# One encoder layer on one core: another way of starting it, with the norm's gain spread by the matrix engine, loads from two queues, and another order of casts, copies and transposes

## The chip, the cores and the metric

The kernel runs on one core of a Trainium2 chip. A core has five engines that each work through an instruction stream of their own, in order: PE (TensorE, matrix multiplication), DVE (VectorE), ACT (ScalarE), POOL (GpSimd) and SP (SyncE, which here only issues DMA transfers; ACT can issue them too). They are tied together by semaphores: an instruction can wait until another engine, or a transfer, has counted up. PE reads operands from the on-chip memory SBUF and writes to the accumulator banks in PSUM; DVE and ACT read PSUM, and POOL in this kernel works in SBUF alone. The metric is the device time of one execution in microseconds (us), the median of the runs.

## The reference

One layer over a sequence of 1024 tokens of width 1024, all in float32. What matters here is its beginning:

```python
h = rmsnorm(x, g_mix)          # x / sqrt(mean(x*x) + eps) * g, for each token
z = h @ w_in                   # columns: 512 pooling | 1024 q | 1024 k | 1024 v
y_pool = pool_mixer(z[:, :512], ...)
y_attn = diff_attention(q, k, v, ...)          # 8 heads
gates  = sigmoid(h @ w_gate + b_gate)
merged = gates[:, :1024] * (y_pool @ w_branch_pool) + gates[:, 1024:] * (y_attn @ w_branch_attn)
x = x + merged @ w_out
x = x + square(relu(rmsnorm(x, g_ffn) @ w_up)) @ w_down
```

Every token needs its normalised row `h` before anything can be multiplied, and head 0 needs its 384 columns of `w_in` (128 each of q, k and v).

## The kernel before

**Digits.** PE multiplies in a rounded float32 form (`F32R`). To keep precision, each operand is held as two tiles, a high digit (the value rounded, by an ACT cast) and a low digit (value minus high digit, by a subtraction on DVE or POOL). `split` (L118) makes the two; `mm3` (L123) multiplies them in three matmuls, L126 high by high, L127 high by low of the weights, L128 low of the activations by high. So each block of weights costs one ACT cast and one subtraction, and each block of activations too.

**Tiles.** The 1024 tokens are eight tiles of 128 (t = 0 to 7). For a tile, `load_x` (L319) brings `x`, `norm_x` (L340) and `norm_transpose` (L262) make `h`: an ACT square with a sum (L277; tile 0 in two halves, ACT L269 and DVE L270), the factor `rs` on DVE and POOL (L259 and L260, L274 and L275 for tile 0), the product `hn` of `x`, `rs` and the gain `g` on DVE in two halves of 512 columns (L281), eight transposes of 128x128 on PE into two banks `hps{t}_0` and `hps{t}_1` (L286), and then four splits into `hT{kp}`, one for each pair kp of K blocks: an ACT cast (L120) and a DVE subtraction (L121) each. The tiles `hT{kp}_{th}_{hl}` hold four token tiles (th is the half of the sequence) and are high (0) or low (1) digits. The gain must be present on all 128 partitions; `gmb` holds it so, loaded by one transfer that repeats the row of 4 KB for each partition.

**Projection.** `stage_qkv` (L430) makes `z{h}_{t}` for head h and token tile t from eight K blocks, three matmuls of 384 columns each: 24 matmuls. The weights of K blocks 2 kp and 2 kp + 1 come as `rqkv{h}_{kp}` in two transfers (`load_w`, L330) and are split by `split_w` (L350) into `wqkv{h}_{k}`. Raw weights of the pool `raw` have two buffers; those with a `u` in the table below take another pool.

**The start.** A table of words, `START`, sets the order in which the program writes down the first loads (x, g, w), norms (n) and splits of weights (s; with a p the subtraction is on POOL, else on DVE). `NX` says at which step g of the main loop the norm of tile t is written down, `LX` the same for its load. The loop runs over 64 pairs of head and tile, with eight stages (A is `stage_qkv`, B to H the attention of earlier tiles, W the weights of the next head). Later, the gate projections (`g{c}_{th}`, 512 columns, weights `fwgate`) and the pooling projections fill in as work for PE.

**Order.** What is written down is a priority list, not the order on an engine: a scheduler simulates the program and puts the ready instruction of the highest priority next, engine by engine. Once built, the order on each engine is fixed, and an engine that waits holds up everything behind it. SP's transfers share eight completion counters in turn, so an issue can also wait for an earlier transfer to land.

Of the kernel before, what the change touches and what calls it, by code (L numbers as in the profile page):

```python
# [42 lines left out]
START = "x0 g n0 w0 w1 w2u w3u x1 s0p s1 x2 s2p s3 x3"  # L43
NX = [-2, -1, 0, 0, 0, 1, 2, 3]
# [13 lines left out]
def encoder_kernel(  # L58
# [42 lines left out]
    hcount = [0]  # L101

# [15 lines left out]
    def split(hi, lo, src, lo_eng=None):  # L118

        nc.scalar.copy(hi, src)  # L120
        (lo_eng or nc.vector).tensor_tensor(lo, src, f(hi), op=ALU.subtract)  # L121

    def mm3(ps, lhs_hi, lhs_lo, rhs_hi, rhs_lo, first, last, more=False):  # L123

        kw = {"skip_group_check": True} if more else {}
        nc.tensor.matmul(ps, lhs_hi, rhs_hi, start=first, stop=False, **kw)  # L126
        nc.tensor.matmul(ps, lhs_hi, rhs_lo, start=False, stop=False, **kw)  # L127
        nc.tensor.matmul(ps, lhs_lo, rhs_hi, start=False, stop=last, **kw)  # L128
# [133 lines left out]
    def norm_transpose(xt, gb, t, dst, hn, small, banks, halves=False):  # L262
# [16 lines left out]
        for j in range(2):  # L279
            js = slice(j * 512, (j + 1) * 512)  # L280
            nc.vector.scalar_tensor_tensor(hn[:, js], xt[:, js], rs, gb[:, js], op0=ALU.mult, op1=ALU.mult)  # L281
            trp, trtag = banks[j % len(banks)]
            ps = trp.tile([P, 512], F32, tag=trtag, name=f"hps{t}_{j}")
            for i in range(4):
                k = 4 * j + i
                nc.tensor.transpose(ps[:, i * P : (i + 1) * P], hn[:, k * P : (k + 1) * P], identf)  # L286
            for i in range(2):
                kp = 2 * j + i
                src = ps[:, i * 256 : (i + 1) * 256].rearrange("p (a b) -> p a b", a=2)
                split(dst[kp, th, 0][:, :, c0 : c0 + P], dst[kp, th, 1][:, :, c0 : c0 + P], src)  # L290

# [8 lines left out]
    with ExitStack() as ph:  # L300
# [9 lines left out]
        xs = {}  # L310
# [9 lines left out]
        def load_x(t):  # L320
            xs[t] = ut([P, D], F32, f"x{t}")
            for c in range(0, D, 512 if t == 0 else D):
                e = c + 512 if t == 0 else D
                nc.sync.dma_start(xs[t][:, c:e], x[t * P : (t + 1) * P, c:e])
# [6 lines left out]
        def load_w(h, kp, raw_fn=raw):  # L331
            rw = raw_fn([P, 2, 384], f"rqkv{h}_{kp}")
            for i in range(2):
                nc.sync.dma_start(
                    rw[:, i, :].rearrange("p (s c) -> p s c", s=3),
                    w_qkv[:, 2 * kp + i, :, h * P : (h + 1) * P],
                )
            raws[h, kp] = rw

        def norm_x(t):  # L340
# [7 lines left out]
            norm_transpose(xs.pop(t), gmb, t, hT, hn, sp, banks, t == 0)  # L348
# [10 lines left out]
        for w in START.split():  # L359
            if w[0] == "x":  # L360
                load_x(int(w[1]))
            elif w[0] == "n":
                norm_x(int(w[1]))
            elif w[0] == "w":
                load_w(0, int(w[1]), utf if w[2:] else raw)
            elif w[0] == "s":
                split_w(0, int(w[1]), nc.gpsimd if w[2:] else nc.vector)
            elif w[0] == "g":
                gmb = ut([P, D], F32, "gmb")
                nc.sync.dma_start(gmb, g_mix[0].partition_broadcast(P))  # L370


        rows = sp.tile([32, P], F32, name="rows")
        nc.gpsimd.memset(rows, 0.0)
# [8 lines left out]
        nc.sync.dma_start(lqk, lambda_qk[0].partition_broadcast(P))  # L383

# [45 lines left out]
        def stage_qkv(h, t):  # L430
# [4 lines left out]
            for k in range(NK):  # L435
# [3 lines left out]
                mm3(z[:, 0:384], l_hi, l_lo, w[:, 0, :], w[:, 1, :], k == 0, k == NK - 1)  # L439
# [217 lines left out]
        for g in range(-2, N + 8):  # L657
# [3 lines left out]
            for t in range(1, NT):  # L661
                if NX[t] == g:
                    norm_x(t)
# [105 lines left out]
    for _ in range(G_FIRST):  # L769
        next(gate_units)  # L770
# [565 lines left out]
```

## Time and profile before

| | us |
|---|---|
| median of 3 runs (1548.48 to 1549.25) | 1548.9 |
| the profiled execution, its own time | 1548.34 |
| its span, first to last instruction | 1546.6 |
| PE busy | 1526.0 |
| DVE, ACT, POOL busy | 1012.4, 816.5, 350.9 |
| PE idle before its first matmul | 8.94 |

A row of the timeline reads: start in us, length in us, engine, line of the kernel, operation, what is written and from what, shape, how many instructions are merged into the row, and in brackets the idle time of the engine before it with what ended it. A matmul's length in these rows contains its way through the array, so matmuls of 0.33 us can start 0.17 us apart; the distance of starts is what counts. In the table of windows, each engine has its busy time with the number of instructions in parentheses. A group of instructions ends with its total busy time, the mean in ns, and the idle time before them.

### The profile page before, as it was taken

The numbers are of one execution on the slowest core, as the hardware profiler recorded it, in microseconds if no ns is written. First come the engines' busy times: TensorE is split into PE (matmuls) and PEld (weight loads), VectorE is DVE, ScalarE is ACT, GpSimd is POOL, SyncE is SP. The second block draws the span as 40 slices with busy tenths as digits, with TensorE's granted clock in tenths as the row PEclk, the third lists the DMA queues.
The fourth block names the chain that finished last, engine by engine and source line by source line (L and its number), as shares of the span: only waits on it lengthen the run. The fifth ranks groups of instructions, "written<-read, shape, count | busy, mean of one in ns | idle before, by whom it ended". The sixth has DMA issues, their size and how long they took to land.

```text
span 1546.6 us, 22053 instructions
## 1 busy us (share of the span) xinstructions
PE 1526.0 (99%) x7649; PEld 1320.4 (85%) x7649; DVE 1012.4 (65%) x2268; ACT 816.5 (53%) x1808; POOL 350.9 (23%) x448
## 2 busy tenths in 40 slices
PE   7999999999999999999999999999999999999999
PEld 6899999999998989888888887888888788888887
DVE  7777777777878787865322448766666668556672
ACT  6656555666666565566432546565555634333331
POOL 6433334243525262315443400000000000000000
PEclk9999999999999999999999999999999999999999
DMA  7111212020202031547426534555432789537650
GB/s 230 49 54 48 64 39 73 20 79 32 81 28 84 28 96 42 177 132 250 139 93 205 177 105 124 180 172 176 137 136 109 259 312 389 196 123 256 225 192 28
DMA packets 166681, 206.41 MB, mean 133 GB/s; under 512 B 10069, under 2 KB 102954, under 8 KB 166570
## 3 DMA queue, kind: packets, MB, share of 16 engines
q1 hardware_dynamic: 149162, 177.71, 34.8%
q10 hardware_dynamic: 17408, 27.30, 4.7%
q8 instruction: 60, 0.98, 0.3%
q14 instruction: 51, 0.42, 0.1%
HBM read 150.42 MB, written 54.56 MB: 133 GB/s over the span
## 4 chain that ended last, share of the span: by engine, by line
PE 91%; DVE 3%; issue 2%; ACT 1%; DMA 1%; POOL 1%; SPq 1%; POOLq 0%; DVEq 0%; ACTq 0%
PE z L126 5%; PE z L128 5%; PE z L127 5%; PE Da L126 4%; PE Da L127 4%; PE Da L128 4%; PE g L126 3%; PE g L127 3%; PE g L128 3%; PE Db L126 3%; PE Db L127 3%; PE Db L128 3%; PE X L126 2%; PE X L128 2%; PE X L127 2%; PE sc L512 2%
## 5 line engine op out<-in xcount | busy, mean ns | idle before, releaser
L126 PE MATMUL z<-wqkv,hT 128*128 128x384 f32 x512 | 174.5, 341 | 0.4 <-DVE qn L453 0.3
L128 PE MATMUL z<-wqkv,hT 128*128 128x384 f32 x512 | 174.1, 340 | 0.0
L127 PE MATMUL z<-wqkv,hT 128*128 128x384 f32 x512 | 173.8, 339 | 0.0
L522 ACT ACTIVATE s<-s,nm 128x256 f32<-128x256 f32 (+7 forms) x128 | 99.6, 778 | 45.8 <-DVE nm L514 42.7
L260 POOL TENSOR_TENSOR ms<-ms,mhalf 128x4 f32<-128x4 f32 x64 | 66.5, 1039 | 158.0 <-DVE ms L259 136.7
L126 PE MATMUL g<-hT,fwgate 128*128 128x512 f32 x256 | 101.0, 395 | 0.1
L127 PE MATMUL g<-hT,fwgate 128*128 128x512 f32 x256 | 101.0, 395 | 0.0
L128 PE MATMUL g<-hT,fwgate 128*128 128x512 f32 x256 | 101.0, 395 | 0.0
L126 PEld LDWEIGHTS z<-wqkv,hT 128*128 128x128 f32 x512 | 96.8, 189 | 3.9 <-DVE qn L453 1.0
L127 PEld LDWEIGHTS z<-wqkv,hT 128*128 128x128 f32 x512 | 96.6, 189 | 3.0
L128 PEld LDWEIGHTS z<-wqkv,hT 128*128 128x128 f32 x512 | 96.6, 189 | 2.2 <-DVE hT L121 0.5
L514 DVE CUSTOM_DVE_ANT_0 s<-sc,dist 128x512 f32<-128x512 f32 (+3 forms) x128 | 74.7, 586 | 19.7 <-PE sc L512 18.2
L121 POOL TENSOR_TENSOR wqkv<-rqkv,wqkv 128x384 fp32r<-128x384 f32 x60 | 64.0, 1085 | 19.2 <-ACT wqkv L120 15.5
L121 DVE TENSOR_TENSOR AS<-s,AS 128x512 fp32r<-128x512 f32 x64 | 43.9, 688 | 35.8 <-ACT AS L120 35.6
L511 PE MATMUL sc<-K,Q 128*128 128x512 f32 (+2 forms) x192 | 66.6, 353 | 0.1
L512 PE MATMUL sc<-K,Q 128*128 128x512 f32 (+2 forms) x192 | 66.5, 354 | 0.0
L459 POOL TENSOR_TENSOR qn<-qn,ggh 128x128 f32<-128x128 f32 x64 | 32.3, 505 | 138.7 <-DVE qn L453 127.7
L485 ACT CAST Q<-tk 64x128 fp32r<-64x128 f32 x128 | 33.2, 259 | 57.8 <-DVE Q L484 56.0
L482 ACT CAST Q<-tk 64x128 fp32r<-64x128 f32 x128 | 33.0, 258 | 53.7 <-DVE K L481 52.3
L121 POOL TENSOR_TENSOR fwgate<-frgate,fwgate 128x512 fp32r<-128x512 f32 x32 | 44.5, 1394 | 51.9 <-ACT fwgate L120 51.8
L128 PEld LDWEIGHTS g<-hT,fwgate 128*128 128x128 f32 x256 | 48.1, 188 | 8.6
L126 PEld LDWEIGHTS g<-hT,fwgate 128*128 128x128 f32 x256 | 48.2, 188 | 7.3 <-ACT go L757 0.4
(430 smaller groups left out, 4640.7 us busy)
## 6 DMA issues: line engine op xcount, KB each, us to landing
wd<-in_w_down_dram SPq DMA_DIRECT2D x56, 512.0 KB, 5.3
wu<-in_w_up_dram SPq DMA_DIRECT2D x32, 512.0 KB, 4.5
udS<-us SPq DMA_DIRECT2D x64, 256.0 KB, 2.4
ur<-udS SPq DMA_DIRECT2D x32, 512.0 KB, 3.3
rqkv<-in_w_in_dram SPq DMA_DIRECT2D x64, 192.0 KB, 2.7
ud<-u ACTq DMA_DIRECT2D x48, 256.0 KB, 2.1
ur<-ud SPq DMA_DIRECT2D x24, 512.0 KB, 4.7
frgate<-in_w_gate_dram SPq DMA_DIRECT2D x32, 256.0 KB, 2.6
```

Of the source, the lines that this page charges most:

```text
L121: (lo_eng or nc.vector).tensor_tensor(lo, src, f(hi), op=ALU.subtract)
L126: nc.tensor.matmul(ps, lhs_hi, rhs_hi, start=first, stop=False, **kw)
L127: nc.tensor.matmul(ps, lhs_hi, rhs_lo, start=False, stop=False, **kw)
L128: nc.tensor.matmul(ps, lhs_lo, rhs_hi, start=False, stop=last, **kw)
L260: nc.gpsimd.tensor_tensor(dst, dst, mhalf[:, :n], op=ALU.pow)
L459: nc.gpsimd.tensor_tensor(qn[:, 2:4, :], qn[:, 2:4, :], ggh.unsqueeze(1).broadcast_to([P, 2, HD]), op=ALU.mult)
L482: nc.scalar.copy(q_hi, q)
L485: nc.scalar.copy(Q[other, m, 1, :], q)
L511: nc.tensor.matmul(dst, Q[:, i, 0, :], rhs, start=True, stop=False)
L512: nc.tensor.matmul(dst, Q[:, i, 1, :], rhs, start=False, stop=True)
L514: nc.vector.tensor_tensor_reduce(out=s[i][:, c : c + w], in0=sc[:, 0:w], in1=dist[:, o0 + c : o0 + c + w], scale=2.0 ** -(h + 1), scalar=B ...
L522: nc.scalar.activation(s[i][:, 0:n], s[i][:, 0:n], AF.Exp, bias=last, scale=-1.0, accum_out=Z[:, i, t : t + 1])
```

## The change

The start table is new: `w1` is loaded through ACT's queue, `w2` into the raw pool, `n0` is written down before `w0`, the low digits of `w0`, `w1` and `w2` are all made on POOL, and those of `w3` on DVE. The first half of x of tile 0 stays on SP's queue, the second goes to ACT's. The norms of tiles 1 to 7 are written down at steps 1, 1, 2, 2, 2, 3, 3 where they were at -1, 0, 0, 0, 1, 2, 3.

The gain comes as one row of 4 KB into one partition, over ACT's queue. Two plain float32 matmuls with a column of ones (one row deep, 512 columns each) spread it over the partitions into two PSUM banks. Tile 0 takes the gain from there; two DVE copies afterwards fill `gmb` for the other tiles.

`tc.issue_after(ins)` adds an order: what is written inside the block and runs on `ins`'s engine stands behind `ins` on that engine (it waits for no completion). With it, tile 0's norm stands behind ACT's loads, the copies to `gmb` behind the low digit of the first pair of `hT`, the splits of weights other than `w0` behind the high digit of that pair, the norms of tiles 1 to 3 behind the last matmul of the projection written down before, and the small parameters and the first gate weights behind the last load of the start.

```diff
-START = "x0 g n0 w0 w1 w2u w3u x1 s0p s1 x2 s2p s3 x3"
-NX = [-2, -1, 0, 0, 0, 1, 2, 3]
+START = "x0 g w1ua n0 w0 w2 x1 w3u s0p s1p s2p x2 s3 x3"
+NX = [-2, 1, 1, 2, 2, 2, 3, 3]
...
-            nc.vector.scalar_tensor_tensor(hn[:, js], xt[:, js], rs, gb[:, js], op0=ALU.mult, op1=ALU.mult)
+            nc.vector.scalar_tensor_tensor(hn[:, js], xt[:, js], rs, gb[j], op0=ALU.mult, op1=ALU.mult)
...
-                nc.sync.dma_start(xs[t][:, c:e], x[t * P : (t + 1) * P, c:e])
+                queue = nc.scalar if t == 0 and c else nc.sync
+                issued[queue] = queue.dma_start(xs[t][:, c:e], x[t * P : (t + 1) * P, c:e]).ins
...
+            gb = g_ps if t == 0 else [gmb[:, 0:512], gmb[:, 512:D]]
+            norm_transpose(xs.pop(t), gb, t, hT, hn, sp, banks, t == 0)
+            if t == 0:
+                with tc.issue_after(marks["hTl"]):
+                    for j in range(2):
+                        nc.vector.tensor_copy(gmb[:, j * 512 : (j + 1) * 512], g_ps[j])
...
+                with tc.issue_after(issued[nc.scalar]):
+                    norm_x(int(w[1]))
             elif w[0] == "w":
-                load_w(0, int(w[1]), utf if w[2:] else raw)
+                load_w(0, int(w[1]), utf if "u" in w else raw, nc.scalar if "a" in w else nc.sync)
             elif w[0] == "s":
-                split_w(0, int(w[1]), nc.gpsimd if w[2:] else nc.vector)
+                with ExitStack() as behind:
+                    if w[1] != "0":
+                        behind.enter_context(tc.issue_after(marks["hT"]))
+                    split_w(0, int(w[1]), nc.gpsimd if w[2:] else nc.vector)
             elif w[0] == "g":
                 gmb = ut([P, D], F32, "gmb")
-                nc.sync.dma_start(gmb, g_mix[0].partition_broadcast(P))
+                g_row = ut([1, D], F32, "g_row")
+                nc.scalar.dma_start(g_row, g_mix)
+                g_ps = [pool.tile([P, 512], F32, tag=tag, name=f"g_ps{tag}") for pool, tag in ((ps_o, "o"), (ps_f, "f"))]
+                for j, ps in enumerate(g_ps):
+                    nc.tensor.matmul(ps, f(ones)[0:1, :], g_row[:, j * 512 : (j + 1) * 512], start=True, stop=True)
...
                 if NX[t] == g:
-                    norm_x(t)
+                    with ExitStack() as behind:
+                        if t < 4:
+                            behind.enter_context(tc.issue_after(marks["z"]))
+                        norm_x(t)
```

All else is the same code, but the scheduler's order differs from here through the attention stage, down to roughly two thirds of PE's instructions; behind that it is the same. Three places are shown. In names, the last number is a buffer's, the ones before it are as above.

ACT after the projection of tile 0 (`sq` and `V` take `z0_0`; `hps1` are the transposes of tile 1; an ACTIVATE that reads `x` is a tile's square and sum). Before:

```order
L448 ACTIVATE sq0_0_428<-z0_0_369 128x256
L120 CAST hT0_0_0_147<-hps1_0_252 128x2x128
L120 CAST hT2_0_0_151<-hps1_1_262 128x2x128
L277 ACTIVATE hn3_301,ss3_302<-x3_223 128x1024
L120 CAST hT1_0_0_149<-hps1_0_252 128x2x128
L277 ACTIVATE hn4_335,ss4_336<-x4_271 128x1024
L120 CAST V0_0_365<-z0_0_369 128x128
```

and of the change:

```order
L469 ACTIVATE sq0_0_349<-z0_0_264 128x256
L121 CAST V0_0_260<-z0_0_264 128x128
L121 CAST hT0_0_0_155<-hps1_0_300 128x2x128
L427 ACTIVATE ls_245<-ls_245 128x2
L121 CAST hT2_0_0_159<-hps1_1_310 128x2x128
L278 ACTIVATE hn3_385,ss3_386<-x3_230 128x1024
L412 ACTIVATE dist_242<-di_345 128x1024
L278 ACTIVATE hn4_419,ss4_420<-x4_252 128x1024
L121 CAST hT1_0_0_157<-hps1_0_300 128x2x128
```

Between the casts of pairs 2 and 1 of tile 1 (`hT2`, `hT1`) stood one square; now two squares and the distance table `dist` stand there.

SP's transfers at the start, the rows that stand ahead of tile 2's x. Before:

```order
L334 DMA rqkv0_2_189<-in_w_in_dram 128x3x128 x2
L334 DMA rqkv0_3_192<-in_w_in_dram 128x3x128 x2
L324 DMA x1_195<-in_x_dram 128x1024
L324 DMA x2_209<-in_x_dram 128x1024
L324 DMA x3_223<-in_x_dram 128x1024
```

and of the change, with the semaphores that each waits for:

```order
L338 DMA rqkv0_2_196<-in_w_in_dram 128x3x128 [waits DMAHW0_49]
L338 DMA rqkv1_0_854<-in_w_in_dram 128x3x128 [waits DMAHW2_49,DMAHW4_49,DMAHW1_49,Pool_49]
L338 DMA rqkv1_0_854<-in_w_in_dram 128x3x128
L328 DMA x1_199<-in_x_dram 128x1024 [waits DMAHW3_49]
L338 DMA rqkv0_3_201<-in_w_in_dram 128x3x128
L338 DMA rqkv0_3_201<-in_w_in_dram 128x3x128 [waits DMAHW5_49]
L328 DMA x2_222<-in_x_dram 128x1024 [waits DMAHW6_49]
```

The first weights of head 1 (`rqkv1_0`) now stand ahead of tile 1's x and of the last weights of head 0. They reuse the raw buffer of `rqkv0_0`, and wait on POOL for the second subtraction that reads it.

POOL at the start, of the change (before, the subtractions of K blocks 0, 1, 4 and 5 stood there):

```order
L276 TENSOR_TENSOR rs0_165<-rs0_165,mhalf_98 128x1
L122 TENSOR_TENSOR wqkv0_0_204<-rqkv0_0_193,wqkv0_0_204 128x384
L122 TENSOR_TENSOR wqkv0_1_207<-rqkv0_0_193,wqkv0_1_207 128x384
L122 TENSOR_TENSOR wqkv0_2_210<-rqkv0_1_152,wqkv0_2_210 128x384
L122 TENSOR_TENSOR wqkv0_3_213<-rqkv0_1_152,wqkv0_3_213 128x384
L122 TENSOR_TENSOR wqkv0_4_216<-rqkv0_2_196,wqkv0_4_216 128x384
L122 TENSOR_TENSOR wqkv0_5_219<-rqkv0_2_196,wqkv0_5_219 128x384
L261 TENSOR_TENSOR rs1_295<-rs1_295,mhalf_98 128x1
```

Six subtractions stand between the factors of tile 0 and of tile 1, where four stood.

29 lines of the change are left out of this document (18 added, 11 removed).

## The prediction, made before the changed kernel was run

> **What bounds the kernel now.** I read the busy shares, the chain of waits and PE's list of waits first, then windows and timeline of the first 45 us.
>
> ```profile
> PE 1526.0 (99%) x7649; PEld 1320.4 (85%) x7649; DVE 1012.4 (65%) x2268; ACT 816.5 (53%) x1808; POOL 350.9 (23%) x448
> PE 91%; DVE 3%; issue 2%; ACT 1%; DMA 1%; POOL 1%; SPq 1%; POOLq 0%; DVEq 0%; ACTq 0%
> PE hps L286 <- DVE hn L281: 9.6, 2, 8.9
> 5.00:10.00 5.00, 1.06 (x5) 1.07 (x6) 1.55 (x3) 1.27 (x3) 1.35 (x2) 1.00 0.98 295
> 10.00:15.00 5.00, 5.00 (x22) 4.73 (x21) 4.41 (x8) 4.30 (x11) 4.30 (x4) 1.00 1.03 368
> 15.00:20.00 5.00, 4.37 (x27) 3.35 (x25) 3.98 (x12) 3.77 (x10) 2.61 (x5) 1.00 0.88 268
> 20.00:25.00 5.00, 5.00 (x31) 4.77 (x30) 4.76 (x15) 3.72 (x11) 3.42 (x6) 1.00 1.03 311
> ```
>
> PE carries 91% of the chain. Its idle time over the span is 1546.6 - 1526.0 = 20.6 us, and 9.6 us of that are two waits for `hn` in the first 17 us. The change touches those, so what counts is by when PE has done a given piece of work. From 20 us on PE is full; what it is late by there, nothing later gives back.
>
> ```profile
> 3.41 0.63 ACT L269 ACTIVATE hn<-x 128x512 f32<-128x512 f32 x1 [1.39 <-DMA x<-in_x_dram]
> 5.29 0.56 POOL L275 TENSOR_TENSOR rs<-rs,mhalf 128x1 f32<-128x1 f32 x1 [3.03 <-DVE rs L274]
> 8.13 1.41 DVE L281 SCALAR_TENSOR_TENSOR hn<-x,rs,gmb 128x512 f32<-128x512 f32 x2 [3.00 <-DMA gmb<-in_g_mix_dram]
> 8.94 1.97 PE L286 MATMUL hps<-identf,hn 128*128 128x128 f32 x8 [8.94 <-DVE hn L281]
> 10.17 0.36 ACT L120 CAST hT<-hps 128x256 fp32r<-128x256 f32 x1
> 13.01 0.52 PE L127 MATMUL z<-wqkv,hT 128*128 128x384 f32 x1
> 13.33 0.47 PE L128 MATMUL z<-wqkv,hT 128*128 128x384 f32 x1
> 16.11 0.34 PE L128 MATMUL z<-wqkv,hT 128*128 128x384 f32 x1
> 17.07 1.23 PE L286 MATMUL hps<-identf,hn 128*128 128x128 f32 x8 [0.63 <-DVE hn L281]
> 21.02 0.44 PE L128 MATMUL z<-wqkv,hT 128*128 128x384 f32 x1
> 23.02 0.17 PE z L126
> 35.45 0.44 PE hps L286 x4
> ```
>
> Tile 0's factor is ready at 5.85, the spread gain at 8.13. The projection of tile 0 runs at 0.32 us a step until 13.3 (13.01 to 13.33) and later at 0.17, as the chain's piece at 23.02 has it (four transposes are 0.44 there); its last matmul starts at 16.11. The row at 21.02 is my mark: the third matmul of K block 2 of tile 1, when 24 transposes and 33 projection matmuls have been issued.
>
> **The start of the new order.** ACT issues four transfers ahead of its table load and the square.
>
> ```profile
> 0.73 1.28 ACT L269 ACT_TABLE_LOAD   x1 [0.73 <-PEq L1322]
> L750 ACTq DMA_DIRECT2D p_dram<-yps x8: 326/327/327, 320.4 to 607.9; - x8
> 2.12 0.43 SPq L334
> ```
>
> At 0.33 (ACT's row) to 0.43 (SP's weights) each and gaps of 0.05, the table load begins at 2.1 to 2.7 and ends at 3.4 to 4.0. I take 3.7, after x has landed (3.41 before). The square and all behind it up to rs took 3.41 to 5.85, of which the wait for DVE's half was 0.5; so rs is there at 5.6, which saves 0.2. The gain: no row shows a plain float32 matmul of 512 columns. From below, the slow projection step, 0.32 us for 384 columns, gives 0.43; from above, the eight transposes, 1.97 / 8 = 0.25 for 128 float32 columns, give 1.0. I take 1.0, as the operands are of that type. The row lands behind x's second half, at about 4.1 (0.7 after the first half's 3.41); the two banks are ready at 5.1 and 6.1, hidden behind rs. So `hn` runs from 5.65 and the transposes from about 6.5 instead of 8.94: a **lead of 2.4 us**. The Trainium skill, FP8 and Floating Point Precision, TensorE Precision Notes, says that true float32 takes four passes through the array; an estimate from that page, 4 x 0.43 = 1.7 us each, puts the banks at 5.8 and 7.5 and takes 1.1 us off the lead. No run here shows it.
>
> The cast of the first `hT` pair follows four transposes: 6.5 + 1.0 + 0.4 = 7.9, the projection begins there (10.53 before, by the row of that cast).
>
> **What paces tile 0's projection.** Each K block needs its low weight digits.
>
> ```profile
> L121 POOL TENSOR_TENSOR wqkv<-rqkv,wqkv x60: 1001/1019/1497, 9.2 to 553.9; 128x384 fp32r<-128x384 f32 x60
> L121 DVE TENSOR_TENSOR wqkv<-rqkv,wqkv 128x384 fp32r<-128x384 f32 x4 | 3.2, 808 | 0.8 <-ACT wqkv L120 0.8
> L120 ACT CAST wqkv<-rqkv 128x384 fp32r<-128x384 f32 x8 | 4.0, 518 | 4.6 <-DMA rqkv<-in_w_in_dram 4.5
> L281 DVE SCALAR_TENSOR_TENSOR hn<-x,rs,gmb 128x512 f32<-128x512 f32 x10 | 7.2, 762 | 3.7 <-DMA gmb<-in_g_mix_dram 3.0 <-POOL rs L260 0.7
> ```
>
> POOL takes 1.0 to 1.3 us for one, DVE 0.8. The two that move cost DVE 1.6 us less and POOL 2 to 2.6 us more. POOL's first two follow rs: 5.6 to 7.7 (at 1.02) or 8.2. The other four wait for ACT's casts, which the explicit order puts behind `hT`: first cast done at 8.4, four subtractions to 12.5 to 13.5, tile 1's factor 0.55 behind. That is slower than PE (0.52 a block at 0.17 a step), but not last: x of tile 1 is.
>
> SP is blocked from its fifth weight transfer on until POOL's second subtraction ends (7.7 to 8.2), since head 1's weights stand there for the same buffer; queued behind are x1, the last weights of head 0, x2, x3, the small parameters and all later loads. After two issues of 0.48, x1 is issued at about 8.8, against 9.12 before.
>
> ```profile
> 9.12 1.45 SPq L324 DMA_DIRECT2D x<-in_x_dram  x3
> 14.17 1.06 ACT L277 ACTIVATE hn<-x 128x1024 f32<-128x1024 f32 x1 [0.70 <-DMA x<-in_x_dram]
> DMA to landing us min/median/max: 4.5/5.0/5.7
> ur<-udS SPq DMA_DIRECT2D x32, 512.0 KB, 3.3
> ```
>
> An x takes 4.5 us or more with the queue full, and 512 KB took 3.3 in the median where it was emptier. The queue now drains while SP waits (512 KB of repeated gain are gone too), so I take 3.6: x1 lands at 12.4; bounds 12.0 and 13.8. The Trainium skill, DMA: Bandwidth & Descriptors, Issuing engines are not separate DMA queues, says that a second issuing engine only saves issue time, as all transfers share 16 engines; the trace agrees in that their share is 0.98 and 1.03 between 5 and 15 us, and by that rule ACT's queue is worth its three or four issues of 0.4 us, nothing in bandwidth.
>
> ```profile
> L277 ACT ACTIVATE hn<-x 128x1024 f32<-128x1024 f32 x6 | 6.4, 1070 | 0.9 <-DMA x<-in_x_dram 0.9
> L277 ACT ACTIVATION_READ_ACCUMULATOR hn<-x 128x1 f32 x6 | 1.2, 197 | 0.0
> L120 ACT CAST hT<-hps 128x256 fp32r<-128x256 f32 x15 | 5.2, 381 | 1.1 <-PE hps L286 1.1
> 22.09 1.09 ACT L391 ACTIVATE dist<-di 128x1024 f32<-128x1024 int32 x1
> L121 DVE TENSOR_TENSOR hT<-hps,hT 128x256 fp32r<-128x256 f32 x14 | 5.4, 413 | 0.0
> ```
>
> The square of x1 now stands on ACT ahead of the last `hT` cast and of the casts of the last weights: 12.4 + 1.27 (square) + 0.38 + 0.52 = 14.6; DVE then 0.6 (low digit of block 6), 1.42 (`hn` of tile 1), 0.6 (block 7): 17.2. The last matmul of tile 0 starts at about **17.45, against 16.11**. The lead is spent and 1.3 us lost (bounds: 0.7 with x1 at 12.0 and quick subtractions, 2.7 with x1 at 13.8).
>
> **Tile 1.** Transposes follow at once (17.6 to 18.5). On ACT: `sq` and `V` 0.6 after the projection's end at 17.8, `hT0` to 18.8, `ls` and `hT2` to 19.4, then two squares (2 x 1.27) and `dist` (1.09) to 23.0, `hT1` to 23.4. PE has only two K blocks (1.0 us) and tile 2's transposes (0.9) for that stretch. On DVE the low digit of `hT1` stands behind tile 4's factor and tile 3's `hn`: 23.0 + 0.15 + 1.42 + 0.41 = 25.0. The mark is reached at **25.05 instead of 21.02**: 4.0 later, less two matmuls of tile 2 done ahead (0.35): 3.7.
>
> **Later.** Before, PE still lost time up to 44 us, at tile 7's transposes ahead of tile 4's projection.
>
> ```profile
> 42.40 0.38 PE L471 MATMUL tk<-identf,qn 128*128 128x128 f32 x2
> 42.94 0.66 PE L286 MATMUL hps<-identf,hn 128*128 128x128 f32 x4 [0.16 <-DVE hT L121]
> 43.74 0.44 PE L126 MATMUL z<-wqkv,hT 128*128 128x384 f32 x1
> PE ta L567 <- DVE AT_0l L121: 0.9, 1, 0.9
> PE ta L567 <- DVE AT_4l L121: 0.6, 1, 0.6
> ```
>
> Six transposes at 0.44 for four, 0.66 us, fill 42.40 to 43.74, so 0.7 us are lost there. The change puts the transposes of tiles 6 and 7 behind tile 4's 24 matmuls, which cover them: -0.7. The two gain matmuls lie in idle PE time; the two `gmb` copies (nearest: 0.76 each) run on DVE while ACT casts weights, and would cost 1.5 without that cover. The reordered attention stage: PE's two longest waits there are 0.9 and 0.6; a new draw may remove or double them, -1 to +2; I take 0.
>
> **Sum**: +3.7 - 0.7 = +3.0 us. The profiled execution took 1548.34 (span 1546.6 and 1.7 around it), so 1551.3; the median of the runs lies 0.6 above it: **1551.9**.
>
> **Rivals.**
> 1. *The lead survives*: every step behind tile 0's transposes moves up with them. For it: 512 KB less ahead of the weights and of x1. Against: SP's wait on POOL, and ACT's order at tile 1. Then 2.4 and 0.7 are gained: 1545.8. It decides if the mark is reached at 18.6, for which SP's wait must end some 3 us sooner than I have it. I leave it more than its steps give, since x1's landing and the gain matmuls, on which all later steps stand, have no row of their own.
> 2. *The new order of the attention stage costs more*: the same delays in many heads, each 0.5 us, less than the rows of `ta` show; eight such waits are +4, with the begin's 3.0: 1555.9. Against: POOL and DVE have slack there.
> 3. *Nothing changes*: x1 lands at 11 to 11.5, and what ACT's order then costs is about the lead: 1549.0. Its landing there needs a transfer faster than the 3.3 of the row.
> 4. *The slow step stays.* Before, steps were 0.32 us for the first 4.4 us of matmuls. Now PE works in pieces until 25 us; if the slow step holds through the 16 matmuls behind the mark, 16 x 0.15 = 2.4 more: 1554.3. The Trainium skill, TensorE: Matmul & The Clock Gate, Part 1, has this rule: half clock until about 3.4 us of sustained work. The trace agrees at 13.3 us, though its granted clock reads 1.00 throughout.
>
> **How the numbers follow.** Forecast 0.48, rivals 0.17, 0.16, 0.13, 0.06. A measurement of this kernel tells about 0.2% (3.1 us) from no change, so slower means above 1552.0. Half of the forecast's own range (1550 to 1553.8) is above: 0.25, with rivals 2 and 4: slower 0.47. Faster is rival 1: 0.17. Within: 0.36. The range 1545.2 to 1556.2 takes in the rivals' times and the bounds of x1's landing, and leaves out the outer half of rivals 1 and 2.
>
> **What would show it.** Right: x1 landing at 12 us or later, SP's wait for POOL's `wqkv`, PE idle between 19 and 25 us, the mark near 25. Wrong: the mark before 22, or a difference that arises behind 50 us.

## The result, and the profile after

The changed kernel takes **1560.6 us** (median of 6 runs, 1559.5 to 1564.4) against 1548.9 (6 runs, 1547.7 to 1549.4): a ratio of 1.0081, 95% interval 1.0068 to 1.0094, so 11.7 us slower. The forecast was 1551.9 with a range up to 1556.2. The profiled execution is the slowest of the six, 1564.4, so the rows below show more loss than the median has.

The page's busy times and PE's share of the chain, of the changed kernel:

```profile
PE 1536.9 (98%) x7653; PEld 1324.5 (85%) x7653; DVE 1001.5 (64%) x2268; ACT 822.3 (53%) x1808; POOL 351.0 (22%) x450
PE 90%; DVE 3%; DMA 2%; issue 2%; ACT 2%; POOL 1%; POOLq 0%; SPq 0%; ACTq 0%; DVEq 0%
```

PE's idle time is 1562.5 - 1536.9 = 25.6 us, 5.0 more than before, but the span grew by 15.9. The other 10.9 us are busy time. The two gain matmuls are 3.7 of them (4.89 to 8.63, a time in which PE is idle in the kernel before). In three stretches the granted clock falls, in the windows from 15 to 25, 970 to 980 and 1245 to 1255 us: 0.94 and 0.72, 0.67 and 0.99, 0.82 and 0.84. With the missing share of each 5 us, an estimate is up to 1.7 us for each stretch. In x1_nx6 below, whose granted clock shows none of the three, PE is busy for 1529.8 us, 3.8 more than before. Waits alone don't account for the loss.

PE's list of waits after the change: engine, tile and line, what it waited for, then total us, number, longest:

```profile
PE g_pso L387 <- DMA g_row<-in_g_mix_dram: 4.9, 1, 4.9
PE X L127 <- ACT AS L121: 2.7, 1, 2.7
PE X L127 <- ACT U L1120: 2.6, 1, 2.6
PE z L127 <- ACT wqkv L121: 1.7, 1, 1.7
...
PE yp L127 <- ACT go L781: 1.4, 2, 0.8
PE z L129 <- DVE hT L122: 1.4, 2, 0.9
PE sc L532 <- DVE nm L535: 1.2, 2, 1.0
PE z L128 <- DVE wqkv L122: 1.2, 2, 1.0
```

The long wait for `hn` is gone, but PE now waits in three other places: for weights and `hT` in the first 28 us, for `go` and `nm` at the attention's end (633 and 645 us), for `AS` and `U` in the feed-forward part (970 and 1247 us). The wait for `U` is not new, only longer; the list before has

```profile
PE X L126 <- ACT U L1094: 1.6, 1, 1.6
```

The timeline of the changed kernel's begin:

```profile
2.78 1.28 ACT L270 ACT_TABLE_LOAD   x1 [2.78 <-issue]
4.46 0.63 ACT L270 ACTIVATE hn<-x 128x512 f32<-128x512 f32 x1 [0.40 <-DMA x<-in_x_dram]
4.89 2.04 PE L387 MATMUL g_pso<-g_row,ones 1*128 1x512 f32 x2 [4.89 <-DMA g_row<-in_g_mix_dram]
6.72 1.91 PE L387 MATMUL g_psf<-g_row,ones 1*128 1x512 f32 x2
8.56 2.03 PE L287 MATMUL hps<-identf,hn 128*128 128x128 f32 x8
1.19 8.04 SPq L338 DMA_DIRECT2D rqkv<-in_w_in_dram  x6
9.27 0.48 SPq L328 DMA_DIRECT2D x<-in_x_dram  x1
15.03 1.06 ACT L278 ACTIVATE hn<-x 128x1024 f32<-128x1024 f32 x1 [2.75 <-DMA x<-in_x_dram]
16.91 0.44 PE L127 MATMUL z<-wqkv,hT 128*128 128x384 f32 x1 [1.74 <-ACT wqkv L121]
19.71 0.52 PE L129 MATMUL z<-wqkv,hT 128*128 128x384 f32 x1
25.94 1.18 ACT L121 CAST hT<-hps 128x256 fp32r<-128x256 f32 x4
27.99 0.44 PE L129 MATMUL z<-wqkv,hT 128*128 128x384 f32 x1 [0.47 <-DVE hT L122]
```

Read it as a chain. Six issues of weights keep SP for 8.04 us, since the fifth waits for a buffer; x of tile 1 is issued at 9.27 and lands at 15.03. ACT stands still for it 2.75 us with the last weights' casts behind; PE waits 1.74 us for those. Tile 0's last matmul starts at 19.71 (16.11 before), the mark at 27.99 (21.02). A gain matmul takes 6.72 - 4.89 = 1.83 us.

Two windows show the transfers around SP's wait (busy us of PE, PEld, DVE, ACT, POOL with instructions, PEclk, DMA share, GB/s):

```profile
8.00:9.00 1.00, 1.00 (x3) 0.44 (x3) 0.33 (x1) 0.00 (x0) 0.30 (x1) 1.00 0.00 0
10.00:15.00 5.00, 4.82 (x21) 4.21 (x19) 2.38 (x5) 2.29 (x7) 3.92 (x4) 1.00 1.04 283
```

While SP waits, the transfers run out. Then they come at once: head 1's weights (384 KB) just ahead of x of tile 1, and the last weights, x2 and x3 within 2.5 us behind it.

**Two marks make the kernels comparable.** The first is the prediction's (third matmul of K block 2 of tile 1). The second is the wait for `u` at the first `Y` product of the feed-forward part, the same instruction with the same wait in every kernel here. Its rows, before and after:

```profile
946.30 0.50 PE L126 MATMUL Y<-B21h,A 128*128 128x512 f32 x1 [0.83 <-DVE u L863]
```

```profile
956.50 0.50 PE L127 MATMUL Y<-B21h,A 128*128 128x512 f32 x1 [0.82 <-DVE u L889]
```

So 10.2 us are lost by there, of which the first mark shows 7.0. In the changed kernel and in those of its variants that have tile 1's order from it, two more projection matmuls stand ahead of the first mark than before (0.35 us); act_order and both_orders have 32 matmuls ahead of it, as before. From the second mark to the end the profiled executions take 1546.6 - 946.30 = 600.3 and 1562.5 - 956.50 = 606.0 us. The table has the same for every kernel that was run; the times are medians, the ratios are to the runs of the kernel before that were taken with them.

| kernel | tile 0's last matmul | first mark | second mark | from there to the end | median | ratio, 95% interval |
|---|---|---|---|---|---|---|
| before | 16.11 | 21.02 | 946.30 | 600.3 | 1548.9 | |
| after | 19.71 | 27.99 | 956.50 | 606.0 | 1560.6 | 1.0068-1.0094 |
| x1_first | 17.33 | 23.90 | 952.78 | 602.3 | 1556.4 | 1.0030-1.0060 |
| cast_first | 17.32 | 27.59 | 957.60 | 600.5 | 1559.3 | 1.0048-1.0078 |
| gain_dma | 15.90 | 22.44 | 958.84 | 600.4 | 1562.8 | 1.0072-1.0103 |
| only_gain | 16.05 | 24.99 | 955.85 | 600.4 | 1556.4 | 1.0027-1.0061 |
| nx6_order | 18.69 | 27.37 | 952.05 | 602.4 | 1555.4 | 1.0025-1.0055 |
| x1_nx6 | 17.36 | 23.94 | 948.23 | 601.4 | 1552.1 | 1.0011-1.0029 |
| act_order | 17.34 | 20.30 | 947.48 | 601.2 | 1551.0 | 1.0005-1.0023 |
| both_orders | 15.97 | 19.98 | 946.97 | 601.3 | 1551.1 | 1.0004-1.0022 |
| x1_nx6_cast | 15.71 | 24.21 | 948.90 | 600.3 | 1550.5 | 1.0006-1.0024 |
| two_queues | 15.10 | 20.81 | 946.10 | 600.5 | 1548.4 | 0.9983-1.0002 |
| two_queues_lam | 15.23 | 20.62 | 946.49 | 600.2 | 1548.4 | 0.9986-1.0004 |
| pool_digits | 17.62 | 22.23 | 947.51 | 600.3 | 1549.0 | 0.9991-1.0010 |
| gain_both | 15.64 | 21.05 | 945.92 | 601.3 | 1550.4 | 1.0002-1.0021 |
| gain_on_act | 21.17 | 26.24 | 951.90 | 602.5 | 1555.3 | 1.0031-1.0058 |

### The profile page after: what moved, and what is told of

It reads as the page before. It is cut to its first block, busy times and chain, and to the rows that moved or that the text cites. A ratio compares the mean times of both kernels' runs of the same rounds, so it can differ in the third digit from the quotient of the medians.

```text
span 1562.5 us, 22102 instructions
## 1 busy us (share of the span) xinstructions
PE 1536.9 (98%) x7653; PEld 1324.5 (85%) x7653; DVE 1001.5 (64%) x2268; ACT 822.3 (53%) x1808; POOL 351.0 (22%) x450
## 4 chain that ended last, share of the span: by engine, by line
PE 90%; DVE 3%; DMA 2%; issue 2%; ACT 2%; POOL 1%; POOLq 0%; SPq 0%; ACTq 0%; DVEq 0%
PE z L127 5%; PE z L129 5%; PE z L128 5%; PE Da L129 4%; PE Da L127 4%; PE Da L128 4%; PE g L127 3%; PE g L129 3%; PE g L128 3%; PE Db L129 3%; PE Db L127 3%; PE Db L128 3%; PE X L127 3%; PE X L129 3%; PE X L128 3%; PE sc L532 2%
## 5 line engine op out<-in xcount | busy, mean ns | idle before, releaser
L535 DVE CUSTOM_DVE_ANT_0 s<-sc,dist 128x512 f32<-128x512 f32 (+3 forms) x128 | 74.7, 586 | 12.7 <-PE sc L533 10.9
```

Source lines behind the costliest of these rows:

```text
L535: nc.vector.tensor_tensor_reduce(out=s[i][:, c : c + w], in0=sc[:, 0:w], in1=dist[:, o0 + c : o0 + c + w], scale=2.0 ** -(h + 1), scalar=B ...
```

## The experiments

### The late x of tile 1

**x1_first.** Head 1's first weights go behind x3 on SP.

```diff
-                    load_w(h, kp)
+                    with tc.issue_after(started):
+                        load_w(h, kp)
```

> The changed kernel with one more order: head 1's first weights are issued on SP behind x of tile 3, so that x of tile 1 doesn't wait for GpSimd's low digits. Theory A (the begin loses its time to the late x of tile 1): x1 lands at 9 to 11 us instead of 15.0, PE's wait of 1.7 us at 15 us goes, the mark (third matmul of K block 2 of tile 1) is reached at 24 to 25 instead of 28.0, and the time is about 1557.5. Theory B (it is lost to the float32 gain matmuls and the low clock that a broken stream of matmuls brings): the mark stays at 27 to 28 and the time at 1560. The order behind the first 130 instructions of PE is the changed kernel's, so waits at about 634, 970 and 1245 us that come again belong to that order or to the phase; if they don't come again they vary from execution to execution.

1556.4 us, and the mark at 23.90. Rows of its timeline, SP and ACT:

```profile
4.84 0.49 SPq L328 DMA_DIRECT2D x<-in_x_dram  x1
11.91 1.08 ACT L278 ACTIVATE hn<-x 128x1024 f32<-128x1024 f32 x1
```

x1 is issued at 4.84 instead of 9.27, and its square has no wait in brackets: the data are there before ACT is. Theory A holds: one order on SP was worth 4.2 us. PE's waits at the attention's end came again at the same instructions (0.84 us for `go`, 0.98 for `nm`), so they are no accident of one execution.

**cast_first.** The casts of the last weights ahead of the square of x1 on ACT.

```diff
                     split_w(0, int(w[1]), nc.gpsimd if w[2:] else nc.vector)
+                    marks["cast"] = marks["hi"]
...
+                            behind.enter_context(tc.issue_after(marks["cast"]))
```

> The changed kernel with one more order: the squares of tiles 1 to 3 stand on ACT behind the casts of head 0's last weights. Theory A (x1 late, and all behind its square with it): PE's wait of 1.7 us for a weight cast at 15 us goes and tile 0's last matmul starts at about 17.7 instead of 19.7, but tile 1's square is 1 us later, so the mark moves by 1 us at most (27 to 28) and the time by 0 to 1 (1559.5 to 1560.6). A rival by which ACT's order alone is the loss: the mark at 25 to 26, the time 1558.

Tile 0's last matmul moves to 17.32 as expected, the mark only to 27.59, the time to 1559.3. Rows of ACT and PE:

```profile
15.30 1.09 ACT L121 CAST wqkv<-rqkv 128x384 fp32r<-128x384 f32 x2 [2.42 <-DMA rqkv<-in_w_in_dram]
19.20 1.23 PE L287 MATMUL hps<-identf,hn 128*128 128x128 f32 x8 [1.55 <-ACT hn L278]
```

The last weights, which stand behind x1 on SP, land no sooner than 15.3, and PE then waits 1.55 us for tile 1's `hn`. Behind SP's wait everything is late; ACT's order mostly decides where it shows first. In this execution the granted clock reads 0.86 from 20 to 25 us and 0.50 from 25 to 30, so a part of the late mark is the clock's and not the order's.

### The gain

**gain_dma.** The changed kernel with the repeating transfer, on ACT's queue.

```diff
-                g_row = ut([1, D], F32, "g_row")
-                nc.scalar.dma_start(g_row, g_mix)
...
+                nc.scalar.dma_start(gmb, g_mix[0].partition_broadcast(P))
```

> The changed kernel with the gain spread by the transfer that repeats the row, on ACT's queue, in place of the two TensorE matmuls and the two copies; head 1's weights then stand behind x3 on SP by themselves. Theory A: hn of tile 0 waits for the gain until 7.5 to 8.5, transposes at 8.5 to 9, the mark within 0.7 us of that of the kernel with x1 first, the time 1556.5 to 1558. Theory B (the matmuls are the loss): the mark is 2 us or more ahead of that kernel's, at 22 or before, and the time 1553 to 1555.

The mark is at 22.44, 1.5 us ahead of x1_first, which has the same order of loads on SP: that is between the two theories, and about the price of the matmul form there. But the time, 1562.8, is the worst of all. Between the two marks it loses 11.1 us more than the kernel before (958.84 - 22.44 against 946.30 - 21.02): its order through the attention stage is another one again, with waits of 1.08 and 2.51 us at 634 and 653 us. The time was a miss of both theories.

**only_gain.** The kernel before with the new gain alone (row on SP's queue, two matmuls, two copies).

```diff
-                nc.sync.dma_start(gmb, g_mix[0].partition_broadcast(P))
+                nc.sync.dma_start(g_row, g_mix)
...
+                    nc.tensor.matmul(ps, f(ones)[0:1, :], g_row[:, j * 512 : (j + 1) * 512], start=True, stop=True)
```

> The kernel before with nothing but the gain spread by TensorE (row of 4 KB on SP's queue, two float32 matmuls, two copies). If the matmuls take 1.8 us each as in the changed kernel, the second bank is ready at 7.5 to 8, transposes begin at 7.5 instead of 8.94, and 0.5 MB less stands ahead of the weights: mark at 19.5 to 20.5 instead of 21.0 and 1547.5 to 1548.5. Theory B (clock): the earlier transposes are followed by waits and a low clock, mark at 21 or later, 1549 to 1551.

Transposes at 7.66, 1.3 us ahead, as expected; then PE waits 1.91 us at 19.96 for `hn` of tile 2, the mark comes at 24.99, and 1556.4 us result: a miss of both theories. The scheduler's order changes here too, from tile 1 on and through the attention stage, where 5.6 us more are lost between the two marks. So this kernel can't tell what the gain alone is worth.

**gain_both.** Tile 0's gain by TensorE, the others' by the repeating transfer behind the last weights, so without the copies.

```diff
-START = "x0 g n0 w0 w1 w2u w3u x1 s0p s1 x2 s2p s3 x3"
+START = "x0 g n0 w0 w1 w2u w3u b x1 s0p s1 x2 s2p s3 x3"
...
+                nc.scalar.dma_start(g_row, g_mix)
```

> The kernel before with the gain spread by TensorE for tile 0 alone (row on ACT's queue); the other tiles' gain still comes by the repeating transfer, behind the last weights, so no copies on DVE, and the attention stage keeps the order of the kernel before. Theory A (the matmuls' 1.8 us each are a small part, a lead of 1 to 1.5 us at tile 0's transposes is real): mark at 20 to 21, 1547.5 to 1549. Theory B (the low clock eats it): mark at 22 or later, 1550 or more.

With the row first on ACT's queue the matmuls begin at 2.56 and are hidden:

```profile
2.56 2.04 PE L375 MATMUL g_pso<-g_row,ones 1*128 1x512 f32 x2 [2.56 <-DMA g_row<-in_g_mix_dram]
4.40 1.91 PE L375 MATMUL g_psf<-g_row,ones 1*128 1x512 f32 x2
7.40 1.11 PE L286 MATMUL hps<-identf,hn 128*128 128x128 f32 x4 [1.09 <-DVE hn L281]
17.12 1.23 PE L286 MATMUL hps<-identf,hn 128*128 128x128 f32 x8 [1.14 <-DVE hn L281]
```

Tile 0's transposes are 1.5 us earlier, those of tile 1 are where they were (17.07 before), and the mark at 21.05: the lead is worth nothing, because x1 sets the next step (its square starts at 14.22 here and at 14.17 before). The median, 1550.4, is above theory A's 1549 and above before, although the second mark is 0.4 us ahead; the part behind it takes 601.3 us. The last pair of experiments says why. The two make 0.6 of the median's 1.5 us; the rest is not explained.

**gain_on_act.** The kernel before with the repeating transfer on the other queue, nothing else.

```diff
-                nc.sync.dma_start(gmb, g_mix[0].partition_broadcast(P))
+                nc.scalar.dma_start(gmb, g_mix[0].partition_broadcast(P))
```

> The kernel before with nothing but the gain's repeating transfer on ACT's queue instead of SP's. This gives the first 50 us a slightly different order, none through the attention stage, and the other order around 946 to 970 us. Theory (the order makes the wait): a wait of 1.7 to 2.7 us for AS at about 960 us, 601.2 us or more from the wait for u to the end, 1549.5 to 1550.5. Rival (the phase): 600.2 to 600.5 us, and 1548.5 to 1549.5. For the begin it tells what a gain by transfer on ACT's queue is worth: transposes of tile 0 at 8.5 to 9.5.

1555.3 us, and the begin was a surprise. Rows of ACT, DVE and PE:

```profile
6.26 0.63 ACT L269 ACTIVATE hn<-x 128x512 f32<-128x512 f32 x1 [3.80 <-DMA x<-in_x_dram]
7.11 0.69 DVE L270 CUSTOM_DVE_ANT_0 hn<-x 128x512 f32<-128x512 f32 x1 [7.11 <-DMA x<-in_x_dram]
10.42 1.11 PE L286 MATMUL hps<-identf,hn 128*128 128x128 f32 x4 [10.42 <-DVE hn L281]
```

The halves of x of tile 0 land at 6.26 and 7.11; before they were there at 3.41 and 4.10, when ACT and DVE began on them. The 512 KB of gain, issued at the same moment on the other queue, are moved beside them: by 6.3 us ACT's queue has moved 0.52 MB. The time was a miss too: theory and rival had 1550.5 at most. One word in one line costs 5 us at the mark.

### The attention stage's order

**nx6_order.** The changed kernel with one number changed. This kernel keeps the changed kernel's order for PE's first 95 instructions, and from about the 140th it has the order of the kernel before on every engine through the attention stage.

```diff
-NX = [-2, 1, 1, 2, 2, 2, 3, 3]
+NX = [-2, 1, 1, 2, 2, 2, 2, 3]
```

> The changed kernel with one number of its table changed: the norm of tile 6 is written down at step 2 instead of 3. The first 95 instructions of PE keep the changed kernel's order, and behind about the 135th every engine has the order of the kernel before through the attention stage. Theory C (part of the loss is the attention stage's new order): the waits at 633 and 645 us (3 us in all, plus about 1 us between 50 and 600 us) go, the difference to before at equal work stays at what the begin left (6 to 7 us), and the time is 1556 to 1557.5. Rival (the waits come from the shifted phase, not from the order): they stay, 1560.

1555.4 us: 5.2 us come back, most of them by an order that nobody wrote down. The begin is the changed kernel's (mark at 27.37, 0.6 earlier); the second mark goes from 10.2 to 5.75 behind, so 3.8 us of the gain lie between the marks, in the attention stage. The window from 600 to 650 us, after and then here (columns as above):

```profile
600.00:650.00 50.00, 47.87 (x261) 41.09 (x260) 39.06 (x114) 30.66 (x88) 20.04 (x27) 1.00 0.43 145
```

```profile
600.00:650.00 50.00, 49.85 (x284) 44.75 (x283) 39.82 (x122) 28.48 (x86) 15.75 (x20) 1.00 0.37 128
```

In the first, PE is idle for 2.1 us of 50, in the second for 0.15. The waits for `go` and `nm` are not in nx6_order's list at all. The rival, that a shifted phase makes these waits, is out: nx6_order arrives there 6 us late too.

**x1_nx6.** Both repairs, this one number and x1_first's line.

```diff
-NX = [-2, 1, 1, 2, 2, 2, 3, 3]
+NX = [-2, 1, 1, 2, 2, 2, 2, 3]
...
-                    load_w(h, kp)
+                    with tc.issue_after(started):
+                        load_w(h, kp)
```

> The kernel with x1 first on SP, with tile 6's norm written down at step 2, which gives it the attention order of the kernel before. Theories A and C together: the begin leaves 2 to 3 us, the attention stage adds nothing: 1551.5 to 1553.5. If the order of the attention stage is no cause: 1556.

1552.1, as forecast from A and C together: the gains of 4.2 and 5.2 us add up to within a microsecond (1560.6 - 9.4 = 1551.2). Against x1_first, which differs in tile 6's norm alone, 4.6 us come back between the marks: the order's price again.

### What is left of the begin

**act_order** puts the squares of tiles 3 and 4 and `dist` behind tile 1's last cast on ACT; **both_orders** also tile 1's norm behind the last low digit of weights on DVE (the first two lines). Both start from x1_nx6.

```diff
+                        if t == 1:
+                            behind.enter_context(tc.issue_after(marks["w"]))
+                        if t in (3, 4):
+                            behind.enter_context(tc.issue_after(marks["t1"]))
...
+                with tc.issue_after(marks["t1"]):
+                    distances()
```

> The kernel with x1 first and tile 6's norm at step 2, with the squares of tiles 3 and 4 and the distance pattern put behind tile 1's last activation cast on ACT. Theory (ACT's order at tile 1 is a term of the loss): PE's waits of 0.66 us for a cast at 22.3 and 0.44 us for a low digit at 23.9 go, the mark moves from 23.9 to about 22.5, the time from 1552.1 to about 1551. Rival (tile 2's or 3's transposes come late instead and take it back): the same time, 1552.

> As that, and tile 1's norm on DVE behind the low digit of head 0's last weights. Theory: PE's wait of 1.43 us at 17.1 shrinks to about 0.5 as well, the mark at 21.5 to 22, the time 1550 to 1550.5; what is left against before is the float32 gain matmuls and the later low clock, 0.5 to 1 us. Rival: tile 1's transposes are late by the same, and the time stays at 1551 or more.

The waits of tile 1 go and the mark comes at 20.30 and 19.98, 0.7 and 1.0 us *ahead* of before; yet the second mark is 1.2 and 0.7 behind. PE's rows of the two where it is lost again:

```profile
27.84 0.63 PE L287 MATMUL hps<-identf,hn 128*128 128x128 f32 x4 [1.43 <-DVE hT L122]
```

```profile
27.45 0.63 PE L287 MATMUL hps<-identf,hn 128*128 128x128 f32 x4 [1.36 <-DVE hT L122]
```

The squares that stood in the way at tile 1 are now late for tiles 3 and 4: DVE stood still for 0.88 us for one of them in both kernels (until 23.03 and 22.57), which may account for a part of PE's wait; what the rest comes from is not shown. act_order gave 1.1 us, the second order nothing that the medians show: half a hit, half the rival.

### Parts of the change on the kernel before, its order held

In the three kernels of this part PE's order is that of before to the last instruction.

**two_queues.** x0's second half and the second weights on ACT's queue.

```diff
+                queue = nc.scalar if t == 0 and c else nc.sync
...
+START = "x0 g n0 w0 w1a w2u w3u x1 s0p s1 x2 s2p s3 x3"
```

> The kernel before with nothing but two loads moved to ACT's queue (the second half of x of tile 0 and the second pair of weights). PE's order is that of the kernel before to the last instruction. Theory (two queues save issue time alone, and ACT's table load starts some 1.2 us later): nothing at the mark, 20.5 to 21.5, 1548.5 to 1549.5. Rival (a second queue brings data earlier): gain and x1 land 1 us earlier, 1547.5. Rival (ACT's issues hold the square): tile 0's factor 1 us later but hidden behind the gain, 1549 to 1550.

```profile
6.72 1.41 DVE L281 SCALAR_TENSOR_TENSOR hn<-x,rs,gmb 128x512 f32<-128x512 f32 x2 [1.27 <-DMA gmb<-in_g_mix_dram]
7.52 1.97 PE L286 MATMUL hps<-identf,hn 128*128 128x128 f32 x8 [7.52 <-DVE hn L281]
17.75 0.35 DVE L405 TENSOR_TENSOR lp<-lqk 128x128 f32<-128x128 f32 x1 [0.68 <-DMA lqk<-in_lambda_qk_dram]
18.50 0.44 PE L128 MATMUL z<-wqkv,hT 128*128 128x384 f32 x1 [0.75 <-DVE hT L121]
```

The old gain, with x on two queues, lets the transposes begin at 7.52, a microsecond sooner than the changed kernel with its matmuls. Of its lead over before, 1.4 us, 1.0 is still there at tile 1's transposes (16.04 against 17.07), for x of tile 1 is earlier too; the waits of DVE and PE at 17.75 and 18.50 take most of the rest. The mark keeps 0.2 us and the median, 1548.4, is not told apart from before. **two_queues_lam** puts `lp`, which held DVE here, behind tile 1's first low digit:

```diff
+                with tc.issue_after(marks["lo", 1, 0]):
+                    lam()
```

> The kernel before with the two loads on ACT's queue and one more order: the product for lambda, which waited 0.68 us on DVE for its transfer, stands behind the low digit of tile 1's first pair. Theory: PE's wait of 0.75 us at 18.5 goes, the difference to before at equal work goes from 0 to -0.5 or -0.9, and the time is 1547.6 to 1548.2, which could be below both kernels. Rival: hn of tile 2 behind it is late by the same 0.7 us and the time stays at 1548.4.

The rival held: 1548.4, and PE waits later instead, 0.44 us for `hn` at 19.1 and 0.86 us for a low digit of `hT` at 26.8. No version clearly below the kernel before was found.

**pool_digits.** The second pair's low digits on POOL (GpSimd).

```diff
-START = "x0 g n0 w0 w1 w2u w3u x1 s0p s1 x2 s2p s3 x3"
+START = "x0 g n0 w0 w1 w2u w3u x1 s0p s1p x2 s2p s3 x3"
```

> The kernel before with nothing but the low digits of the second pair of weights on GpSimd instead of DVE; PE's order is that of before. GpSimd makes six in a row at 1.0 us or more instead of four, from 9.2: theory (GpSimd paces tile 0): its last low digit ends at about 15.3 and the block that needs it starts then, the mark 0.5 to 1.5 us later than 21.0, 1549.5 to 1550.5. Rival (x of tile 1 ends later than that, or PE works at the rows' 0.32 us a step anyway): no change, 1548.9.

PE waits twice 0.49 us for POOL and both marks are 1.2 us later in the profiled execution, but the median is 1549.0 with an interval of 0.9991 to 1.0010. What the digits cost is below what these runs can tell.

### The wait in the feed-forward part

Of the fourteen kernels so far (without gain_on_act), seven take 600.2 to 600.5 us behind the second mark and seven, the changed kernel among them, 601.2 or more. The longer ones have another order around 945 to 970 us, the same in all of them. **x1_nx6_cast** (x1_nx6 with cast_first's edit) takes it away; gain_on_act, above, brings it into the kernel before.

```diff
+                            behind.enter_context(tc.issue_after(marks["cast"]))
```

> The kernel with x1 first and tile 6's norm at step 2, with the squares of tiles 1 to 3 behind the casts of head 0's last weights on ACT. Its order from 50 us on is that of the kernel before, around 946 to 970 us too, where the kernel without this edit has the other order. Theory (the order makes the wait): no wait of over 1 us for AS at 960 us, 600.2 to 600.5 us from the wait for u to the end instead of 601.4, and about 1 us less than 1552.1 if the begin stays within half a microsecond. Rival (the phase makes it): the wait of about 2.2 us stays, 601.2 us or more.

Both went by the order: 600.3 us without it, 602.5 with it. Not all of the 2.2 us is the order's: those of the longer kernels that have 602.3 to 602.5 (x1_first, nx6_order, gain_on_act) show a lowered granted clock right behind the second mark (0.75 to 0.89 in the window from 950 to 955 us), those at 601.2 to 601.4 none. So about 1 us is the order's. ACT's rows of x1_nx6 and then of x1_nx6_cast:

```profile
957.46 0.62 ACT L121 CAST BT4h<-y 128x512 fp32r<-128x512 f32 x1 [2.27 <-DVE y L893]
958.06 0.63 ACT L1101 ACTIVATE u<-u 128x512 f32<-128x512 f32 x1
958.72 0.63 ACT L1102 ACTIVATE u<-u 128x512 f32<-128x512 f32 x1
959.38 0.33 ACTq L1106 DMA_DIRECT2D ud<-u  x1
959.75 0.59 ACT L1121 COPY U<-X 128x512 f32<-128x512 f32 x1 [0.40 <-ACT u L1102]
960.23 0.59 ACT L1126 COPY z<-Z 128x512 f32<-128x512 f32 x1
960.71 0.63 ACT L121 CAST AS<-s 128x512 fp32r<-128x512 f32 x1
```

```profile
957.45 0.62 ACT L121 CAST BT4h<-y 128x512 fp32r<-128x512 f32 x1 [1.55 <-DVE y L895]
959.55 0.62 ACT L121 CAST AS<-s 128x512 fp32r<-128x512 f32 x1 [1.48 <-DVE s L895]
961.12 0.58 ACT L1123 COPY U<-X 128x512 f32<-128x512 f32 x1
```

The cast of `BT4h` starts at the same time in both. In the first, two activations of `u`, the issue of its transfer and two copies stand ahead of the cast of `AS`, which starts 1.16 us later; PE's wait for `AS` is then 2.2 us. In the changed kernel it is 2.7, in x1_nx6_cast none is listed.

## Why the prediction was wrong

- **The table load and the square.** Predicted 3.7 and "after x has landed" at 3.41; the table load ended at 4.06, but x itself landed at 4.46. `rs` was ready at 6.38 and not at 5.6. Its gain of 0.2 us was a loss of 0.5: two_queues, which has ACT's queue in use too, starts its square at 4.24, and only_gain, with all on SP, at 3.33: transfers on the second queue delay the first one, which the sum left out. gain_on_act shows the same effect at its largest. The Trainium skill, DMA: Bandwidth & Descriptors, Issuing engines are not separate DMA queues, says that transfers from all issuing engines run on the same 16 engines and interleave. The trace agrees (x at 6.26 instead of 3.41), and the rule was read in the prediction as "no gain", not as a loss for the first transfer.
- **The gain matmuls.** 1.0 us taken, bounds 0.43 to 1.0; measured 1.83, outside the bounds. The estimate from the Trainium skill, FP8 and Floating Point Precision, TensorE Precision Notes (four passes, 1.7), came near: the trace agrees with 1.83. The row came at 4.89 instead of 4.1, and `hn` waited 1.37 us for the first bank. The lead at tile 0's transposes was 0.4 us, not 2.4.
- **SP's wait, and x1's landing: the failed step of the begin.** The wait was as described (x1 issued at 9.27, predicted 8.8). "I take 3.6: x1 lands at 12.4; bounds 12.0 and 13.8" was wrong: 15.03, 5.76 us after issue. The reason given for 3.6 did come true, for the queue ran empty (DMA share 0.00 from 8 to 9 us). What it left out is that SP's wait holds back transfers that then come together: head 1's 384 KB ahead of x1, 1.4 MB right behind it, a share of 1.04 from 10 to 15 us. The time was that of the trace's rows of 4.5 to 5.7. Tile 0's last matmul was at 19.71, predicted 17.45. x1_first, where head 1's weights are out of x1's way, is 4.2 us faster; what the transfers ahead and behind cost each is not shown.
- **ACT's order at tile 1.** The mechanism was right (`hT1`'s cast at 25.94 stands behind two squares and `dist`), and act_order moved the mark by 3.6 us (3.3 at equal work); but most of it is taken back at 27.8 us, so that the order is worth 1.1 us, and not the 2.7 that the sum had between tile 0's end and the mark.
- **The mark** came at 27.99, predicted 25.05. Less the two matmuls done ahead, the begin lost 6.6 us and not 3.7.
- **Later, -0.7.** In the changed kernel it is not seen as a net gain: new waits of 0.7 us for `Q` (ACT) and 0.5 us for `hT` (DVE), at 53 to 55 us, stand in PE's list. With the attention order of before it is: x1_nx6 is 2.9 us behind at the first mark, 2.6 at equal work, and 1.9 at the second.
- **The attention stage, the step that failed by most.** "A new draw may remove or double them, -1 to +2; I take 0." nx6_order and x1_nx6 show 3.8 and 4.6 us between the marks. Rival 2 had nearly the size (+4), but the wrong form: not half a microsecond in many heads; the largest piece lies in a few waits where the attention stage runs out (2.0 us of PE's time from 600 to 650 us).
- **The feed-forward part** was taken as unchanged. The difference of order reached down to two thirds of PE's instructions, and just there, at 945 to 970 us, it costs about 1 us, and about 2 where the clock falls as well.
- **Rival 4** (the slow step stays) was real in another form: the slow step ended at 12.6 us, but came back behind 19 us, and the granted clock was 0.72 from 20 to 25 us. By the estimate above that is up to 1.7 us, and as much behind each of the two long waits of the feed-forward part; what it cost alone was not measured. (The trace's record of the granted clock begins at 12.6 us here and at 13.6 before, so the 1.00 that windows ahead of that print is no measurement of the slow step at the start.) **Rival 1** had no lead to go by, 0.4 us instead of 2.4; and the leads of 1.5 and 1.4 us at the transposes of gain_both and two_queues leave nothing and 0.2 us at the mark.

The medians go in steps: 1560.6, tile 6's norm a step earlier and with it the old order of the attention stage 1555.4 (-5.2), x1 1552.1 (-3.3), the casts first and with them the old order of the feed-forward part 1550.5 (-1.7). What is left, 2.0 us against the runs of before taken with the last, is the begin's: x1_nx6_cast is 2.6 us behind at the second mark in its profiled execution (where the granted clock reads 0.66 from 20 to 25 us), x1_nx6 1.9 (with 1.00). Which step of the begin these 2 us belong to was not separated. The long wait for `U` at 1247 us (2.6 us, where the other kernels have 1.5 to 1.8) is only in the changed kernel's profiled execution; what made it was not tried.

## What to carry to other kernels

An edit of a few microseconds at the start, under a scheduler that simulates, is judged by the order that it leaves hundreds of microseconds later: compare the built orders first, and test the edit in a form that keeps them. A lead at the first step is worth what the next input allows; ask when x of the next tile lands before counting it. An issue that waits on a queue also bunches the transfers behind it; what stands ahead of the one that is needed next should be something that is needed sooner. A transfer that is moved to a second queue to save issue time starts beside the one that the kernel waits for.

## What the runs showed of the hardware

- 512 KB on a second queue, issued together with the two halves of x, delayed the first half from 3.41 to 6.26 us.
- A float32 matmul of 512 columns out of a single row took 1.83 or 1.84 us (4.89 to 6.72, 2.56 to 4.40), the time of eleven of the projection's later steps of 384 columns at 0.17.
- A wait on PE can cost more than its length. The changed kernel's windows (columns as above) show a granted clock of 0.94 and then 0.72 around waits of 1.7 and 1.0 us, and at 21.6 us two of its matmuls start 0.47 us apart. The third row lies behind its wait of 2.7 us for `AS`. In only_gain, behind a wait of 1.9 us, matmuls go 0.32 us apart from 22.03 to 23.31. x1_nx6 waited 1.4 us until 17.1 us and its clock stayed at 1.00, so not every wait brings it.
- The same waits may or may not bring it. Those of 1.5 and 0.8 us ahead of the second mark are in every kernel here. In ten of the sixteen profiles the granted clock falls there (in two_queues to 0.70 from 945 to 950 us), in six it does not (before: 1.00). What decides is not shown.

```profile
15.00:20.00 5.00, 2.10 (x7) 1.30 (x7) 3.15 (x7) 3.38 (x7) 1.50 (x2) 0.94 0.58 219
20.00:25.00 5.00, 3.85 (x18) 3.01 (x17) 3.07 (x11) 3.37 (x9) 2.34 (x4) 0.72 0.94 358
970.00:975.00 5.00, 4.88 (x14) 3.75 (x15) 4.90 (x9) 3.39 (x7) 0.00 (x0) 0.67 0.55 149
```
